# A two-layer hybrid trunk on one core: a gated delta net's planner costs, gating by halves, the order of Winograd splits and the places of operands

## The chip, the cores and the metric

The program runs on one core of one Trainium2 chip. The metric is the device time of one execution in microseconds. Five engines matter: PE (TensorE, the matrix products; PEld is its loading of the stationary operand), DVE (VectorE), ACT (ScalarE), POOL (GpSimd) and SP (SyncE, which issues most of the DMAs).

## The reference, cut to what matters

The input is a sequence of 1024 rows of 1024 numbers. Two layers are computed, each with a mixer and a feed-forward part, a modulation by a condition vector, and a layer norm after each part:

```python
e = jax.nn.silu(c @ cond_w + cond_b)
for i in range(DEPTH):                       # 2 layers
    mod = (e @ ada_w[i] + ada_b[i])[:, None, :]
    sh1, sc1, g1, sh2, sc2, g2 = jnp.split(mod, 6, axis=-1)
    y = mixers[i % N_MIXERS](x * (1.0 + sc1) + sh1)          # layer 0: gated delta net, layer 1: retention
    x = layer_norm(DN_ALPHA * x + (1.0 + g1) * y, ln_g[i, 0], ln_b[i, 0])
    y = conv_ffn(x * (1.0 + sc2) + sh2, ffn_up[i], ffn_conv_w[i], ffn_conv_b[i], ffn_down[i])
    x = layer_norm(DN_ALPHA * x + (1.0 + g2) * y, ln_g[i, 1], ln_b[i, 1])
```

The gated delta net has 8 heads of 128. Its projections q, k, v pass a short causal convolution and SiLU; q and k are normalised; per chunk a unit lower triangular system is solved, and a scan over the chunks carries a 128 x 128 state:

```python
kk = jnp.where(strict, jnp.einsum('bhncd,bhnmd->bhncm', kb, k) * decay, 0.0)
sol = lax.linalg.triangular_solve(kk + eye, rhs, left_side=True, lower=True, unit_diagonal=True)
v_new = u_n - jnp.einsum('bhck,bhkv->bhcv', w_n, state)
o = q_n * exp(g_n) @ state + qk_n @ v_new
state = state * jnp.exp(g_last)[..., None] + (k_n * exp(g_last - g_n))^T @ v_new
o = o * lax.rsqrt(jnp.mean(o * o, axis=-1, keepdims=True) + 1e-6) * norm_w
o = o * silu(z)                              # the gate; then o @ w_out
```

Retention has 4 heads with rotated q and k, 8 chunks of 128 and a normalisation of its output before a gate. The feed-forward part is `(silu(causal_dwconv(gate) + conv_b) * up) @ w_down` with 2816 hidden units.

## The kernel before, in words

Activations are kept transposed, features on the 128 partitions and time along the row, in two halves of 512. A product of full precision is made of three products of the faster type: each operand is split into a rounded high part (an ACT copy, line 89) and the rest (a DVE subtraction, line 90), by `split` (L88), and `mm3` (L108) or its like adds low times high, high times low and high times high. So each operand tile costs one ACT and one DVE pass before PE can use it. Instructions are emitted in program order, and a scheduler sets the order on each engine, from that order and from a model of when each is ready; only PE's order within `run` is fixed by the kernel itself.

*Delta net (about 80 to 620 us).* `run` (L725) is a planner: streams (Python generators) yield how long to wait on the planner's clock `clk`, or an event, and the ready stream of the lowest number goes next. Each product adds its cost to the clock (`pm`, `ptr`) and is chained behind the last on PE. The waits are in the table `LAT` (L1205). `filler` (L1150) has the last rank and emits the projections, one item of 48 products at a time (c: a tile of q, k or v; s: the same stored to memory for later; z: the gate's). For each quad of heads `t_path` (L843) makes the products `kk` and solves the 32 x 32 diagonal blocks on DVE (31 steps, transposes, three results RX, TX and T); `t_chain` (L913) copies these blocks to `T0` and `R` (by ACT, DVE and POOL) and joins them to 128 x 128 with products of 32 and 64 columns (`t1`, `t2`, `t3`); `prep` (L1006) transposes v and then k (`U`, whose `aux` places are given back after the scan); `dt_half` (L1027) makes the masked products `DT`; `scan` (L1050) goes over 8 chunks per head, four heads side by side, with the waits `s1`, `s2`, `s3`; `tail` (L1104) normalises four chunks, transposes them into `DT`'s tile and stores it to `oTd`. The second quad's `t_path` begins when the first quad's scans are done.

*Gating (L1224).* For each head the stored gate `zd` (512 KB) and both halves of `oTd` are loaded by SP, and DVE multiplies them in place. Then `proj_ln` (L312) makes the output projection, half of the rows at a time, with the weights' loads, four x rows' loads and background work (`bg_step`) as hooks; `bg_ada(0, 5, "row")` puts eight 512 KB loads of a modulation matrix and their DVE sums into that background (L1652).

*Feed-forward, up (L1266, `strassen`).* Weights of 256 columns and the activations are taken as 2 x 2 blocks in Winograd's form (`wino`, L1333): seven products of 12 matmuls each; the sums s1 to s4 of weight blocks are made by DVE in two PSUM banks in turn and each is split before its product. The results go to `sink`s: for the first item the gate with its convolution (`conv_q`, L1694: ACT copy L1699, two DVE sums L1704, ACT SiLU L1705), then the product with up (L1727). The same function makes the retention's q, k and gates, where the sink is the rotation (`rope_item`, 12 DVE operations an item, L1807 to L1812).

*Down projections and retention's output (L1408, `proj_gen`).* Seven products in Winograd's form again; each step `ops` (L1456) splits one activation block `ab` and one weight block `bb` into the tags "wl", "wr", "wh" (two places each) and, where `early`, "hTb". The last two steps of each product are kept as a tail and done by output tile. `early` holds in the first layer's down projection for the first five products, in the second's for all, in the retention's output projection for none.

*Retention (about 1735 to 2110 us).* The same planner runs `ret_v` as filler and `core` and `ret_back` per chunk, with the waits `RL` (L1981).

The lines at the planner's products and at the operands' places are these:

```python
def pm(out, lhsT, rhs, start=True, stop=True, cost=0.216):
    pq(pe.matmul(out, lhsT, rhs, start=start, stop=stop), cost)
...
at = ltags[0] if last and j >= nj - ltags[3] else ("wl", "hTb", "wr")[n % 3] if early else ("wl", "wr")[n % 2]
wt = ltags[1] if last and j >= nj - ltags[2] else ("wh", "hTb", "hTb")[n % 3] if early else "wh"
```

## Time and profile before

| what | value |
|---|---|
| median of 3 runs | 2921.36 us (2917.78 to 2926.29) |
| the profiled execution | 2919.49 us, its span 2917.7 us |
| mean granted clock of PE | 0.987 |
| busy: PE, DVE, ACT, POOL | 2799.6, 2183.0, 1299.3, 494.8 us |
| moved by DMA | 467.40 MB, 160 GB/s on the mean |

The span is from the first to the last instruction. "Busy" of an engine is the union of its instructions' times; matmuls are pipelined, so a busy PE is not at its peak. A wait's row names who waited, for what, the total in us, how often, and the longest. A window's row gives its length and then busy time and count for PE, PEld, DVE, ACT and POOL, then the granted clock of PE, the share of DMA and GB/s. A row of a timeline gives the start, the time it took, engine, line, operation, the tile written and those read, and in brackets the engine's idle time before it and what ended it. Rows of the chain in order of time give start, length and what was worked on.

### The profile page before, as it was taken

The numbers are of one execution on the slowest core, as the hardware profiler recorded it, in microseconds if no ns is written. First come the engines' busy times: TensorE is split into PE (matmuls) and PEld (weight loads), VectorE is DVE, ScalarE is ACT, GpSimd is POOL, SyncE is SP. The second block draws the span as 40 slices with busy tenths as digits, with TensorE's granted clock in tenths as the row PEclk, the third lists the DMA queues.
The fourth block names the chain that finished last, engine by engine and source line by source line (L and its number), as shares of the span: only waits on it lengthen the run. The fifth ranks groups of instructions, "written<-read, shape, count | busy, mean of one in ns | idle before, by whom it ended". The sixth has DMA issues, their size and how long they took to land.

```text
span 2917.7 us, 38768 instructions
## 1 busy us (share of the span) xinstructions
PE 2799.6 (96%) x13594; PEld 2288.3 (78%) x13594; DVE 2183.0 (75%) x3874; ACT 1299.3 (45%) x2387; POOL 494.8 (17%) x509
## 2 busy tenths in 40 slices
PE   8999999999999999998999999999999999999997
PEld 6787887877788788887877877777777788888886
DVE  6796678576789888768677665666688877777779
ACT  4754564444654444545333332222344644444543
POOL 0301311000023232200000022422202023331001
PEclk9998999999999999999999999999999999999999
DMA  7223332274355555855343374755664163434853
GB/s 282 94 79 100 123 127 81 80 255 150 104 170 170 191 182 168 292 163 169 130 148 115 117 241 150 215 169 173 196 220 144 55 201 134 143 128 162 289 181 116
DMA packets 252884, 467.40 MB, mean 160 GB/s; under 512 B 24144, under 2 KB 77776, under 8 KB 252688
## 3 DMA queue, kind: packets, MB, share of 16 engines
q1 hardware_dynamic: 217984, 409.07, 42.5%
q10 hardware_dynamic: 32064, 47.20, 4.4%
q0 software_dynamic: 2640, 8.65, 0.8%
q8 instruction: 107, 1.75, 0.3%
q14 instruction: 89, 0.73, 0.1%
HBM read 347.91 MB, written 116.92 MB: 159 GB/s over the span
## 4 chain that ended last, share of the span: by engine, by line
PE 68%; DVE 16%; DMA 8%; ACT 4%; issue 3%; POOL 1%; SPq 0%; ACTq 0%; DVEq 0%; POOLq 0%
PE acc L714 14%; PE acc L1272 8%; PE acc L110 5%; PE acc L111 5%; PE acc L112 5%; PE sc L1272 4%; PE acc L1570 4%; PE sc L714 4%; PE mm L714 3%; PE sc L110 2%; DVE o L1704 2%; PE sc L111 2%; PE sc L112 2%; DMA mvw<-in_ada_w 2%; DVE wb L90 2%
## 5 line engine op out<-in xcount | busy, mean ns | idle before, releaser
L714 PE MATMUL acc<-hT,wh 128*128 128x512 f32 x960 | 301.8, 396 | 0.0
L1570 PE MATMUL acc<-bb,ab 128*128 128x512 f32 x984 | 237.0, 399 | 14.1 <-DVE bb L90 12.4
L1570 PEld LDWEIGHTS acc<-bb,ab 128*128 128x128 f32 x984 | 186.8, 192 | 58.4 <-DVE bb L90 16.7
L714 PEld LDWEIGHTS acc<-hT,wh 128*128 128x128 f32 x960 | 184.1, 192 | 35.2
L1272 PE MATMUL acc<-T,wb 128*128 128x512 f32 x840 | 203.6, 391 | 8.3 <-DVE wb L90 8.1
L89 ACT ACTIVATE ab<-ar 128x512 fp32r<-128x512 f32 x210 | 130.2, 626 | 174.0 <-PE mm L303 46.5
L714 PE MATMUL acc<-hT,wl 128*128 128x512 f32 x480 | 200.6, 418 | 3.1 <-DVE wl L90 2.0
L90 DVE TENSOR_TENSOR ab<-ar,ab 128x512 fp32r<-128x512 f32 x210 | 147.6, 708 | 64.9 <-ACT ab L89 64.8
L411 POOL TENSOR_TENSOR xg<-xg,gb 128x512 f32<-128x512 f32 x48 | 63.6, 1327 | 772.2 <-DMA xg<-xs 468.7
L1272 PEld LDWEIGHTS acc<-T,wb 128*128 128x128 f32 x840 | 156.6, 188 | 46.2 <-DVE wb L90 11.1
L90 DVE TENSOR_TENSOR wl<-wr,wh 128x1024 fp32r<-128x1024 f32 x98 | 123.4, 1259 | 81.7 <-ACT wh L89 81.3
L89 ACT ACTIVATE wh<-wr 128x1024 fp32r<-128x1024 f32 x98 | 103.7, 1059 | 158.8 <-PE acc L714 60.0
L1735 POOL TENSOR_TENSOR o<-o 128x512 f32<-128x512 f32 x80 | 125.5, 1578 | 285.2 <-PE acc L112 185.2
L90 DVE TENSOR_TENSOR wb<-wr,wb 128x512 fp32r<-128x512 f32 x162 | 115.6, 718 | 71.9 <-ACT wb L89 71.7
L90 DVE TENSOR_TENSOR wb<-mm,wb 128x512 fp32r<-128x512 f32 x216 | 145.8, 684 | 25.3 <-ACT wb L89 24.5
L1704 DVE SCALAR_TENSOR_TENSOR o<-g,vc,o 128x512 f32<-128x512 f32 (+2 forms) x176 | 156.9, 909 | 4.4 <-ACT o L1699 3.8
L89 ACT ACTIVATE wb<-mm 128x512 fp32r<-128x512 f32 x216 | 124.3, 596 | 75.3 <-DVE mm L1326 71.3
L1342 ACT ACTIVATE pc<-acc 128x512 f32<-128x512 f32 x143 | 84.7, 592 | 139.4 <-PE acc L1272 91.4
L89 ACT ACTIVATE wb<-wr 128x512 fp32r<-128x512 f32 x162 | 98.6, 627 | 106.7 <-DMA wr<-in_ffn_up 45.8
L714 PE MATMUL acc<-wh,hT 128*128 128x512 f32 x384 | 135.0, 415 | 1.0 <-DVE vv L90 1.0
L110 PE MATMUL acc<-T,wb 128*128 128x512 f32 x292 | 115.3, 395 | 5.4 <-DVE wb L90 5.4
L239 DVE SCALAR_TENSOR_TENSOR ada<-mvw,e,ada 128x512 f32<-128x512 f32 x140 | 105.4, 753 | 18.2 <-DMA mvw<-in_ada_w 17.9
(671 smaller groups left out, 7375.5 us busy)
## 6 DMA issues: line engine op xcount, KB each, us to landing
wr<-in_ffn_up SPq DMA_DIRECT2D x92, 512.0 KB, 4.2
mvw<-in_ada_w SPq DMA_DIRECT2D x80, 512.0 KB, 4.5
ad<-o SPq DMA_DIRECT2D x154, 256.0 KB, 3.1
ar<-ad SPq DMA_DIRECT2D x154, 256.0 KB, 3.7
Br<-in_ffn_down SPq DMA_DIRECT2D x88, 256.0 KB, 3.4
wr<-in_ret_wv SPq DMA_DIRECT2D x32, 512.0 KB, 4.2
ar<-od SPq DMA_DIRECT2D x56, 256.0 KB, 5.3
wr<-in_gdn_wqkv SPq DMA_DIRECT2D x24, 512.0 KB, 3.5
```

Source lines behind the costliest of these rows:

```text
L89: act.activation(dst_h, src, AF.Copy)
L90: eng.tensor_tensor(dst_l, src, dst_h, ALU.subtract)
L110: mm(acc, wl[:, k], hl[0], start=first, stop=False)
L111: mm(acc, wh[:, k], hl[1], start=False, stop=False)
L112: mm(acc, wh[:, k], hl[0], start=False, stop=last)
L239: dve.scalar_tensor_tensor(a, wr[:, kk], e[:, k:k + 1], a, ALU.mult, ALU.add)
L714: pq(pe.matmul(out, lhsT, rhs, start=start, stop=stop), cost)
L1272: return pe.matmul(*a, skip_group_check=True, **kw)
L1342: act.activation(t, X, AF.Copy)
L1570: return pe.matmul(*args, skip_group_check=True, **kw)
L1704: dve.scalar_tensor_tensor(tv, gv[:, c0 - j:c1 - j], w[:, 2 - j:3 - j], tv, ALU.mult, ALU.add)
L1735: (dve if fp == 0 else pool).tensor_tensor(o[d], o[x], o[y], op)
```

## The change

Six things, in the order of the program:

- In the delta net the planner's costs of a product come from a table by its columns (`COST`), so 512 columns cost 0.229 instead of 0.216 and products of 32 and 64 columns 0.067 and 0.119 instead of 0.028 and 0.056. The retention's planner uses the same `pm`. The waits in `LAT` are changed, `kk` is shorter for the second quad, `prep` waits for the events `T0` of both pairs and then `v`, tails are staggered by head, `aux` is given back one chunk earlier.
- The filler's items stand in another order, and `fetch` loads and splits the weights of the next item before an item's products.
- The gating goes by halves: first all heads' first half, then the second; for heads 4 to 7 the second half is not stored and loaded but read from the tail's tile `DT`. `bg_ada(0, 5, "row")` is registered after the x loads of the first half's projection.
- In `wino` the second sum's split stands ahead of the third sum.
- The operands of `proj_gen` take the six places of "wl", "wr" and "wh" in turn where it is not early.
- In the first convolution of each up projection, the ACT copy is issued behind the newest split's ACT copy.

```diff
     def split(dst_h, dst_l, src, eng=dve):
-        act.activation(dst_h, src, AF.Copy)
+        anchor["sp"] = act.activation(dst_h, src, AF.Copy)
...
-            hooks = hooks + loads
+            hooks = hooks + loads + list(then)
...
-    def pm(out, lhsT, rhs, start=True, stop=True, cost=0.216):
-        pq(pe.matmul(out, lhsT, rhs, start=start, stop=stop), cost)
+    COST = {32: 0.067, 64: 0.119, 128: 0.224, HALF: 0.229}
+
+    def pm(out, lhsT, rhs, start=True, stop=True, cost=None):
+        pq(pe.matmul(out, lhsT, rhs, start=start, stop=stop), cost or COST[out.shape[-1]])
...
-                yield LAT["kk"]
+                yield LAT["kk"] - 0.4 * g
...
     def prep(p):
         heads = pairs[p]
-        yield after_ev(("T", p // 2), *[("f", 2 * GH + h) for h in heads])
+        yield after_ev(("T0", p & 2), ("T0", p | 1), *[("f", 2 * GH + h) for h in heads])
+        yield LAT["v"]
...
                 pm(p5, U[h][:, n], w)
+                if n == NCH - 2:
+                    give("aux", 1)
...
-        yield LAT["tail"]
+        yield LAT["tail"] + h % 4 * 0.8
...
-        act.dma_start(oTd[0][h, :, hs(q4)], flat(d))
+        if not (q4 and p > 1):
+            act.dma_start(oTd[0][h, :, hs(q4)], flat(d))
...
     def filler(items):
-        for kind, ti in items:
+        wnext = []
+
+        def fetch(i):
+            parked = set()
+            for j, (kind, ti) in enumerate(items):
+                if kind == "s":
+                    parked.add(ti)
+                elif kind == "h" or (kind == "c" and ti in parked):
+                    continue
+                if j >= i:
+                    wnext.append(load_w(A["gdn_wz" if kind == "z" else "gdn_wqkv"][ti]))
+                    return
+
+        for i, (kind, ti) in enumerate(items):
...
-            w = load_w(A["gdn_wz" if kind == "z" else "gdn_wqkv"][ti])
+            if not wnext:
+                fetch(i)
+            w = wnext.pop()
+            fetch(i + 1)
...
-    LAT = {"kk": 3.6, "exp": 3.2, "ld": 6.0, "g1": 12.0, "gm": 3.0, "mm": 2.2, "T": 6.0, "X": 3.4, "fs": 4.85, "T0": 8.0, "t1": 2.0, "t2": 3.3, "t3": 1.7, "D": 2.7, "s1": 1.9, "s2": 1.4, "s3": 1.8, "tail": 12.5, "ssq": 9.3, "fv": 4.0}
+    LAT = {"kk": 4.4, "v": 6.0, "exp": 3.2, "ld": 6.0, "g1": 12.0, "gm": 3.2, "mm": 2.2, "T": 6.0, "X": 11.0, "fs": 5.3, "T0": 10, "t1": 3.4, "t2": 3.3, "t3": 3.0, "D": 2.7, "s1": 1.4, "s2": 1.3, "s3": 1.6, "tail": 14.0, "ssq": 9.3, "fv": 4.0}
...
-    items = [("h", 1), ("h", 2), ("h", 3), (c, K + 2), (c, K + 3), (z, 0), (c, V), (c, V + 1), (c, V + 2), (c, V + 3), (c, 1),
-             (s, 2), (s, 3), (s, K + 4), (s, K + 5), (z, 1), (z, 2), (z, 3), (c, K + 4), (c, K + 5), (c, K + 6),
-             (c, K + 7), (s, 6), (s, 7), (c, V + 4), (c, V + 5), (c, V + 6), (c, V + 7), (c, 4), (c, 5),
-             (z, 4), (z, 5), (z, 6), (z, 7)]
+    items = [("h", 1), ("h", 2), ("h", 3), (c, K + 2), (c, K + 3), (z, 0), (s, 2), (c, 1), (s, 3), (c, V + 0), (c, V + 1), (c, V + 2), (c, V + 3), (s, K + 4), (s, K + 5), (z, 1), (z, 2), (c, K + 4), (c, K + 5), (c, K + 6), (c, K + 7), (z, 3), (s, 6), (s, 7), (c, V + 4), (c, V + 5), (c, V + 6), (c, V + 7), (z, 4), (c, 4), (c, 5), (z, 5), (z, 6), (z, 7)]
...
+    def gate_gdn():
+        raws = [two("qkv", F32, "raw") for _ in range(GH)]
+        for hf in range(2):
+            for k in range(0, GH, 2):
+                g = tl("aux", [P, 2, HALF], name="zg")
+                for j in range(2):
+                    sp.dma_start(g[:, j], zd[k + j, :, hs(hf)])
+                for j in range(2):
+                    raw = raws[k + j][hf]
+                    if hf and k + j in quads[1]:
+                        src = DT[k + j, 1]
+                    else:
+                        src = raw
+                        ld = sp.dma_start(raw, oTd[0][k + j][:, hs(hf)])
+                        if not hf:
+                            anchor["x", 0] = ld
+                    dve.tensor_tensor(raw, src, g[:, j], ALU.mult)
         return raws
...
             z5 = copy_of(Z)
+            w2 = block(s2)
             s4 = psub(a12, s2)
             drain(2)
-            prod(s2, "T2", X)
+            prod(None, "T2", X, w2)
...
-            at = ltags[0] if last and j >= nj - ltags[3] else ("wl", "hTb", "wr")[n % 3] if early else ("wl", "wr")[n % 2]
-            wt = ltags[1] if last and j >= nj - ltags[2] else ("wh", "hTb", "hTb")[n % 3] if early else "wh"
+            ring = ("wl", "wr", "wh")
+            at = ltags[0] if last and j >= nj - ltags[3] else ("wl", "hTb", "wr")[n % 3] if early else ring[2 * n % 3]
+            wt = ltags[1] if last and j >= nj - ltags[2] else ("wh", "hTb", "hTb")[n % 3] if early else ring[(2 * n + 1) % 3]
...
-            bg_ada(0, 5, "row")
...
-            xts = proj_ln(0, GH, get, wout, xsrc, G1, ("x", i))
+            xts = proj_ln(0, GH, get, wout, xsrc, G1, ("x", i), then=[lambda: bg_ada(0, 5, "row")])
...
-                act.activation(t, gv[:, hs(hf)], AF.Copy, scale=w[:, 2:3])
+                with after("sp") if fp == 0 else nullcontext():
+                    act.activation(t, gv[:, hs(hf)], AF.Copy, scale=w[:, 2:3])
```

## The prediction

> **What bounds the kernel now.** I read the page first, then the chain that ended last, then the waits of PE, then the stages by windows of time, and the timeline at each larger wait.

> ```profile
> span 2917.7 us, 38768 instructions
> PE 2799.6 (96%) x13594; PEld 2288.3 (78%) x13594; DVE 2183.0 (75%) x3874; ACT 1299.3 (45%) x2387; POOL 494.8 (17%) x509
> PEclk9998999999999999999999999999999999999999
> PE 68%; DVE 16%; DMA 8%; ACT 4%; issue 3%; POOL 1%; SPq 0%; ACTq 0%; DVEq 0%; POOLq 0%
> 813.77 2.72 PE acc L1272 x12
> ```

> PE is the bound: 96% busy, and most of the chain. Twelve 512-wide products in 2.72 us are 0.227 us each; where PE is never late that pace holds for whole stretches. The diff neither removes nor adds a product, so it can only win or lose time in which PE waits, or runs at the half clock that follows some waits. The third view names what PE waits for (total, times, longest).

> ```profile
> PE acc L1570 <- DVE bb L90: 12.4, 10, 4.8
> PE acc L1272 <- DVE wb L90: 8.1, 9, 1.1
> PE acc L717 <- DVE qkv L1014: 5.5, 1, 5.5
> PE acc L110 <- DVE wb L90: 5.4, 2, 2.7
> PE mm L717 <- DVE on L1938: 4.6, 4, 2.6
> PE acc L717 <- ACT sq L509: 4.4, 1, 4.4
> PE mm L714 <- DVE U L872: 2.9, 2, 1.5
> PE acc L714 <- DVE wl L90: 2.0, 2, 1.6
> ```

> The fourth view puts them in stretches: length, then busy time of PE, PEld, DVE, ACT and POOL, then the granted clock. I count as lost a stretch's length less PE's busy time, plus (1 - PEclk) times the length.

> ```profile
> 124.00:140.00 16.00, 11.74 (x59) 9.09 (x58) 13.68 (x54) 10.06 (x13) 3.28 (x4) 1.00 0.27 96
> 170.00:180.00 10.00, 8.42 (x37) 6.63 (x36) 8.32 (x15) 6.22 (x9) 0.18 (x2) 1.00 0.46 145
> 229.00:260.00 31.00, 25.48 (x392) 22.73 (x391) 23.10 (x45) 17.28 (x40) 8.50 (x22) 0.79 0.33 105
> 485.00:500.00 15.00, 10.04 (x105) 8.71 (x106) 11.56 (x20) 7.71 (x25) 4.46 (x9) 0.77 0.33 106
> 596.00:620.00 24.00, 24.00 (x132) 20.19 (x132) 16.27 (x39) 13.70 (x27) 3.02 (x3) 1.00 0.59 200
> 630.00:660.00 30.00, 25.80 (x110) 20.05 (x109) 24.53 (x35) 7.39 (x9) 0.00 (x0) 1.00 0.82 299
> 783.00:798.00 15.00, 11.20 (x42) 8.52 (x41) 13.93 (x24) 8.37 (x14) 0.00 (x0) 0.89 0.32 104
> 1320.00:1350.00 30.00, 25.21 (x106) 20.36 (x105) 24.94 (x53) 10.98 (x18) 4.13 (x4) 0.94 0.53 167
> 1364.00:1390.00 26.00, 22.83 (x100) 18.27 (x99) 22.99 (x39) 15.82 (x28) 0.59 (x1) 0.93 0.27 92
> 1480.00:1735.00 255.00, 248.13 (x1085) 202.60 (x1084) 180.03 (x285) 93.48 (x164) 16.12 (x12) 1.00 0.44 149
> 2036.00:2050.00 14.00, 11.25 (x51) 8.61 (x50) 11.02 (x21) 6.98 (x13) 0.82 (x2) 1.00 0.55 170
> 2110.00:2135.00 25.00, 20.99 (x89) 16.33 (x89) 23.89 (x39) 9.16 (x17) 0.00 (x0) 1.00 1.03 382
> 2185.00:2206.00 21.00, 18.49 (x77) 13.72 (x76) 21.00 (x42) 10.61 (x19) 0.50 (x1) 1.00 0.37 112
> 2305.00:2320.00 15.00, 11.32 (x41) 8.76 (x42) 15.00 (x25) 7.96 (x14) 0.00 (x0) 0.89 0.35 116
> ```

> In order (596 lost nothing) these lose 4.3, 1.6, 12.0, 8.4, 4.2, 5.5, 6.6, 5.0, 6.9, 2.8, 4.0, 2.5 and 5.3 us: 69 us that the change can reach. They are the ground of every term below.

> **The change part by part.**

> *`prep` waits for the `T0` blocks plus 6 us instead of `T`.* Before, its transposes of v (L717) follow directly on T, while ACT, DVE and POOL copy the diagonal blocks:

> ```profile
> 480.67 3.65 DVE L928 COPY R<-RX 32x128 f32<-32x128 f32 x8
> 485.10 2.83 DVE L928 COPY T<-TX 32x256 f32<-32x256 f32 x6
> 489.95 1.11 PE L717 MATMUL acc<-cst,qkv 128*128 128x128 f32 x4 [5.55 <-DVE qkv L1014]
> ```

> L1014, which must empty the accumulators, stands in DVE's queue behind both copy groups. The stretches at 229 and 485 lose 20.4 us; the idle part is 10.5, the rest half clock. Later transposes find DVE free, and filler products cover the copies. What is late next: the filler's own accumulators, which ACT frees. The scan is not delayed: v needs 6 + 4 x 2.2 planner us, less than `T0` plus `t1`, `t2`, `t3`. Ends 0 and -20.4; I take -12, since the small products at 247 stay.

> *`kk` 3.6 to 4.4 (4.0 in the second quad), `gm` 3.0 to 3.2.* More filler before the products that wait for L872 and L828; ends 0 and -4.3, taken -2.

> *`fetch` loads the next item's weights one item early.* Same loads and splits, moved ahead of one item of 48 products; the wait on wl is 2.0 us. A split that now stands ahead of a step of the chain in DVE's queue delays it by its own length. Ends +2 and -2, taken -1.5.

> *Gating by halves, last halves straight from `DT`, and the row of `ada` after the x loads.* 24 SP issues become 28 (zg halves, four raw loads fewer), 16 stores on ACT's queue become 12. SP's own issuing is 0% of the chain, so four more issues cost nothing while the filler lasts; without it each delays the load behind it. From 596 to 620 PE is busy 24.00 of 24.00, so gating earlier wins nothing there. The loss is behind it, 4.2 us at 630, where weights of the output projection wait behind loads of ada on SP:

> ```profile
> 631.63 8.70 DMA mvw<-in_ada_w
> ```

> Moving eight such loads back frees the weights; they meet later weights instead. Ends +4 and -4.2, taken -3.

> *The convolution's ACT copies behind the newest split (`after("sp")`).* At both starts of the Winograd part the convolution is ahead of the first sum's split:

> ```profile
> 783.93 1.40 DVE L1704 SCALAR_TENSOR_TENSOR o<-g,vc,o 128x512 f32<-128x512 f32 x2
> 785.26 0.68 DVE L90 TENSOR_TENSOR wb<-mm,wb 128x512 fp32r<-128x512 f32 x1
> 785.99 0.68 PE L110 MATMUL acc<-T,wb 128*128 128x512 f32 x1 [2.71 <-DVE wb L90]
> ```

> The stretches at 783 and 2305 lose 10.8 us together. Without L1704 ahead the split comes 1.4 us or more earlier, and the half clock after the wait goes too. Queued behind the new wait on ACT: L1699, and then the gate product L1727, which is needed later. Ends 0 and -10.8, taken -8. [...]

> *Six operand places in turn.* Only "not early" steps use it: the last two products of the first layer's down projection, and the whole retention output projection. Before, `bb` has two places ("wh"), both held by the tail of a product, so the next split on ACT waits for PE:

> ```profile
> 1339.39 0.63 ACT L89 ACTIVATE bb<-Br 128x512 fp32r<-128x512 f32 x1 [8.23 <-PE acc L1570]
> ```

> After, both operands have three; `ab` goes from four to three. In the first the stretches at 1320 and 1364 lose 11.6 us: ends +3 and -11.6, taken -8. In the second those at 2036, 2110 and 2185 lose 9.3: the first is partly DVE's queue of the retention, so -5 of ends +3 and -9.3.

> *Second sum's split ahead of the third sum.*

> ```profile
> ACT wb L89 <- DVE mm L1326: 71.3, 68, 2.6
> 1605.51 3.02 PE L1272 MATMUL sc<-T,wb 128*128 128x512 f32 x12 [1.06 <-DVE wb L90]
> ```

> ACT's split waits 68 times for a sum, and in the retention's projections (1480 to 1735) the second sum's product is late after rope items: 6.9 us. With the split first, DVE's part can go before the rope's operations. Ends +7 and -6.9, taken -5. [...]

> *Staggered tails (14 + 0.8 per head instead of 12.5), `aux` given back one chunk earlier, the filler's new order.* Nothing: filler products hide them (24.00 of 24.00 at 596). Without that cover the last tail, 16.4 planner us, would lie open behind the last scan; its price is in the slower rival.

> *Planner's costs.* These shift the order of PE in two stages.

> ```profile
> L714 PE MATMUL acc<-hT,wh 128*128 128x512 f32 x960 | 301.8, 396 | 0.0
> 609.54 0.39 PE L714 MATMUL mm<-w,DT 128*128 128x128 f32 x2
> 618.23 0.40 PE L714 MATMUL acc<-hT,wl 128*128 128x512 f32 x1
> ```

> A filler product costs 0.227 us; the planner takes 0.229 instead of 0.216. In the retention its waits `b`, `c` and `p` (6.51 us a chunk) are unchanged, so each chunk has 5.7% or 0.37 us less cover, at most 12 us over 32 chunks. There PE already waits for `on` 4.6 us in 4 places. Ends -1 and +12; taken +4.

> In the delta net a quad's waits on the chain add up, old: `kk` 28.8, `X` 3.4, `fs` 48.5, `T` 6, `T0` 8, `t1` to `t3` 7, `mm` 2.2, scan 37.1 = 141 planner us, or 148 real (x 0.227/0.216). New: 35.2 + 11 + 53 + 6 + 10 + 9.7 + 2.2 + 31.4 = 158.5, or 157 real; the second quad 154. So the chain grows by 15 us. The last scan ends at 609.5 and filler lasts to 618.5: 9 us of room, 6 short. Rounding each of 94 waits to a whole filler step of 0.69 us moves this both ways. Ends -9 and +60, taken +5, because after the filler the scan runs at its own pace.

> Sum: -12 -2 -1.5 -3 -8 -8 -5 -5 +4 +5 = -35.5 us. The profiled execution took 2919.5 us (span 2917.7 and 1.8 around it), 1.9 below the median of 2921.4. So 2884 on its scale, and 2886 on the median's.

> **The rivals.**

> *Waits move instead of going.* In the stretches of the sums, the ring and the convolution DVE is busy 13.93 of 15, 15.00 of 15 and 21.00 of 21 us: there it is the bound, and another order of its queue only makes another operand late (the third sum after the second). Then the 26 us of these four terms keep a quarter: -35.5 + 19.5 = -16, 2905 us. Against it: in the 255 us of 1480 DVE is busy only 180, and at 1339 it was ACT that waited, for a buffer.

> *All of it goes.* The 69 us less 9: -60, 2861 us. Against it: half clock after small products, and DVE full at three places.

> *The change does not do what it says:* the new order on DVE and ACT loses elsewhere what the waits gave, and it stays at 2921 within 8.

> *Slower: the filler runs out.* Place: the last scans, 560 to 620. If 94 waits are each rounded up by two thirds of a step, the chain grows by 43 more; 15 + 43 - 9 = 49 us idle, with clock lost as at 485 (0.23) 60 us in place of +5: -40.5 + 60 = +20, 2941 us. It decides from an overrun of 40 us on. For it: 1440 filler products (960 with wh, half as many with wl) are all there is. Against: scan waits shrink, and the first half of the projection can now follow before the second halves are done.

> **How the numbers follow.** A measurement here tells about 0.3% (9 us) from no change. Chances: forecast 0.50, waits move 0.22, all goes 0.08, no change 0.08, filler runs out 0.12. Faster 0.80, same 0.08, slower 0.12. The range reaches from all of it to no change, 2862 to 2922, and leaves out the slower case and half of the fastest. The likeliest case's own range is 2871 to 2901.

> **What would show it.** PE's waits on L1014 and on `sq` before L717 gone, the clock near 1.00 there; the waits on wb at L110 below 1 us; PE's waits on `bb` at L1570 under 5 us from 12.4; those on wb at L1272 under 4. Wrong would be: PE idle between the last scan product and the first L326, new waits on wb under L1272 with "22" operands, many waits on `on` or `Sr` in the retention.

## The result, and the profile after

The changed kernel takes 2905.0 us (median of 7) where the kernel before takes 2921.7: a ratio of 0.9946, 95% interval 0.9932 to 0.9960. A second set of runs gave 0.9963 (0.9952 to 0.9974). It is faster by 0.4 to 0.5%, 11 to 16 us, where 35.5 were forecast. The direction and the range held; the size did not. The profiled execution after took 2897.4 us, 7.6 below its median, so that a comparison of the two profiles alone flatters the change.

The first two lines of the page after:

```profile
span 2895.6 us, 38913 instructions
PE 2794.7 (97%) x13594; PEld 2284.7 (79%) x13594; DVE 2184.7 (75%) x3874; ACT 1295.0 (45%) x2387; POOL 490.4 (17%) x509
```

PE is still the bound. What it waits for after (total, times, longest):

```profile
PE acc L719 <- ACT oq L488: 5.5, 1, 5.5
PE acc L110 <- DVE wb L90: 4.2, 5, 1.6
PE acc L1285 <- ACT pc L1355: 4.0, 5, 1.7
PE acc L1585 <- DVE bb L90: 2.5, 1, 2.5
PE acc L716 <- ACT sq L509: 2.4, 1, 2.4
PE acc L1285 <- DVE wb L90: 2.2, 4, 1.1
PE mm L282 <- DMA xlo<-xs: 2.0, 1, 2.0
```

The announced rows went: bb 12.4 to 2.5, wb in the Winograd products 8.1 to 2.2, the 5.5 us on L1014 (now L1017) to 1.1. The row of wb at L110 only spread, 5.4 us in two waits to 4.2 in five with a longest of 1.6. In their place stand rows that the kernel before did not have or hardly had: 5.5 us at the transposes of the first quad on ACT's L488, 2.0 us on the loads of xlo, 4.0 us on ACT's pc. The same stretches as before, shifted to where their products stand now (length, busy PE, PEld, DVE, ACT, POOL, granted clock):

```profile
124.00:140.00 16.00, 13.76 (x69) 10.90 (x68) 14.52 (x50) 6.86 (x10) 4.19 (x5) 1.00 0.36 115
155.00:170.00 15.00, 12.16 (x60) 10.12 (x60) 12.80 (x41) 11.05 (x36) 2.32 (x3) 0.89 0.17 55
173.00:183.00 10.00, 10.00 (x50) 8.38 (x49) 7.59 (x18) 7.26 (x25) 3.12 (x5) 1.00 0.39 120
232.00:263.00 31.00, 25.52 (x223) 21.82 (x222) 26.11 (x47) 18.74 (x30) 9.94 (x21) 0.89 0.49 160
481.00:492.00 11.00, 11.00 (x52) 9.13 (x51) 8.89 (x17) 10.05 (x17) 9.82 (x22) 1.00 0.17 53
492.00:527.00 35.00, 31.46 (x457) 27.35 (x457) 19.48 (x42) 11.84 (x39) 0.18 (x1) 0.80 0.19 62
629.00:656.00 27.00, 26.53 (x116) 21.25 (x115) 23.28 (x33) 7.25 (x9) 0.00 (x0) 1.00 0.60 202
777.00:789.00 12.00, 10.75 (x47) 8.17 (x46) 11.39 (x20) 9.25 (x17) 0.00 (x0) 1.00 0.19 55
1466.00:1716.00 250.00, 246.90 (x1085) 202.97 (x1083) 178.99 (x286) 91.55 (x161) 17.13 (x12) 1.00 0.45 150
1716.00:1835.00 119.00, 112.79 (x500) 88.24 (x500) 66.02 (x108) 32.70 (x51) 35.90 (x37) 0.97 0.61 191
```

The convolution's start lost 5.5 us and now 1.25; the head of the output projection 4.2 and now 0.5; the retention's projections 6.9 and now 3.1. The stretch right behind those projections loses 6.2 + 0.03 x 119 = 9.8 us; before it lost 4.1 + 0.01 x 115 = 5.2 (row below). The stretch at 485 is clean where it lost 8.4, and the one behind it, at 492, now loses 3.5 + 0.20 x 35 = 10.5, before (500 to 535) 1.3 + 0.10 x 35 = 4.8. Over the whole delta net the granted clock did not gain: its stretches at one half add up to 34.1 us between 80 and 620 before, and to 34.1 in both profiles of the changed kernel.

```profile
1735.00:1850.00 115.00, 110.93 (x500) 86.76 (x499) 63.51 (x108) 31.88 (x50) 34.84 (x36) 0.99 0.59 184
```

Seventeen more kernels were run, and the changed one again. Each left a profile, so what a part does in a stage can be read over several executions. For the table I took, product by product in PE's order, the time from one end to the next less a pace for its shape (0.227 us for 512 columns, 0.111 for an instruction of 128, 0.06 for 64, 0.026 for 32; from one end to the next the profile of before has medians of 0.227, 0.111 and 0.058 and, for 32, a mean of 0.025), and added it over a stage, between the same products in every kernel. "Without" and "with" are means over the kernels that lack or have that part; the number of kernels is in brackets.

| stage (times of before) | forecast | without | with | found |
|---|---|---|---|---|
| delta net, 79-620 | -10.5 | 48.3 (7) | 51.6 (5) | +3.3 |
| output projection, 620-712 | -3 | 12.4 (5) | 7.2 (4) | -5.2 |
| two starts of the convolution | -8 | 12.4 (7) | 3.8 (7) | -8.6 |
| rest of the two feed-forward parts | 0 | 14.9 (6) | 14.9 (5) | 0 |
| down projection, 1320-1390 | -8 | 11.2 (7) | 7.8 (7) | -3.4 |
| retention's projections, 1480-1735 | -5 | 10.3 (8) | 3.2 (6) | -7.1 |
| retention's run | +4 | 15.9 (7) | 24.2 (2) | +8.3 |
| retention's output | -5 | 13.4 (7) | 9.2 (7) | -4.2 |
| norm and start behind it, 2206-2306 | 0 | 11.5 (7) | 12.3 (7) | +0.8 |
| sum | -35.5 | | | -16 |

The sum agrees with the time of the first set. Single profiles of one group differ (by 6 to 7 us in the delta net, by 5 in the down projection), so a row of 3 us is not far above chance. The missing 19 us are in three rows, the delta net (14), the down projection (5) and the retention's run (4), less 4 that the others won beyond their terms.

### The profile page after: what moved, and what is told of

Same layout as the page of the kernel before. It is cut to its first block, busy times and chain, and to the rows that moved or that the text cites. A ratio compares the mean times of both kernels' runs of the same rounds, so it can differ in the third digit from the quotient of the medians.

```text
span 2895.6 us, 38913 instructions
## 1 busy us (share of the span) xinstructions
PE 2794.7 (97%) x13594; PEld 2284.7 (79%) x13594; DVE 2184.7 (75%) x3874; ACT 1295.0 (45%) x2387; POOL 490.4 (17%) x509
## 4 chain that ended last, share of the span: by engine, by line
PE 54%; DVE 23%; DMA 10%; issue 6%; ACT 5%; POOL 1%; SPq 0%; ACTq 0%; DVEq 0%; POOLq 0%
PE acc L716 9%; PE acc L1285 5%; PE acc L1585 4%; PE acc L110 4%; PE acc L111 4%; PE acc L112 4%; PE sc L716 3%; PE sc L1285 3%; DVE o L1719 3%; PE mm L716 2%; DMA mvw<-in_ada_w 2%; DVE wb L90 2%; DMA wr<-in_ffn_up 2%; DVE qkv L490 2%; DVE mm L1339 2%
## 5 line engine op out<-in xcount | busy, mean ns | idle before, releaser
L1585 PE MATMUL acc<-bb,ab 128*128 128x512 f32 x984 | 230.9, 393 | 6.9 <-DVE ab L90 3.3
L89 ACT ACTIVATE ab<-ar 128x512 fp32r<-128x512 f32 x210 | 131.1, 629 | 220.9 <-PE mm L303 48.3
L90 DVE TENSOR_TENSOR ab<-ar,ab 128x512 fp32r<-128x512 f32 x210 | 149.0, 715 | 81.4 <-ACT ab L89 81.3
L1285 PE MATMUL acc<-T,wb 128*128 128x512 f32 x840 | 202.1, 389 | 0.4 <-DVE wb L90 0.4
L89 ACT ACTIVATE wb<-mm 128x512 fp32r<-128x512 f32 x216 | 124.1, 597 | 167.3 <-DVE mm L1339 158.8
L90 DVE TENSOR_TENSOR wl<-wr,wh 128x1024 fp32r<-128x1024 f32 x98 | 123.3, 1258 | 82.8 <-ACT wh L89 82.5
L89 ACT ACTIVATE wh<-wr 128x1024 fp32r<-128x1024 f32 x98 | 103.6, 1060 | 148.3 <-PE acc L716 60.1
L90 DVE TENSOR_TENSOR wb<-wr,wb 128x512 fp32r<-128x512 f32 x162 | 114.1, 705 | 64.1 <-ACT wb L89 64.0
L1750 POOL TENSOR_TENSOR o<-o 128x512 f32<-128x512 f32 x80 | 112.5, 1414 | 269.0 <-ACT pc L1355 175.2
L90 DVE TENSOR_TENSOR wb<-mm,wb 128x512 fp32r<-128x512 f32 x216 | 145.2, 686 | 6.9 <-ACT wb L89 6.9
L1339 DVE TENSOR_TENSOR mm<-wr 128x512 f32<-128x512 f32 x108 | 87.8, 813 | 76.7 <-DMA wr<-in_ffn_up 61.3
L89 ACT ACTIVATE wb<-wr 128x512 fp32r<-128x512 f32 x162 | 101.3, 626 | 94.0 <-PE acc L1285 28.4
```

Of the source, the lines that this page charges most:

```text
L89: anchor["sp"] = act.activation(dst_h, src, AF.Copy)
L90: eng.tensor_tensor(dst_l, src, dst_h, ALU.subtract)
L1285: return pe.matmul(*a, skip_group_check=True, **kw)
L1339: dve.tensor_tensor(t, x, y, op)
L1585: return pe.matmul(*args, skip_group_check=True, **kw)
L1750: (dve if fp == 0 else pool).tensor_tensor(o[d], o[x], o[y], op)
```

## The experiments

Ratios are to the kernel before, run on the same chip, with 95% intervals; 0.001 is 2.9 us.

**Three late parts together, and each alone.** Edit: the kernel before with the convolution's copies behind the newest split (first two pairs of lines), the second sum's split in front of the third sum, and the six operand places; then with each of the three alone.

```diff
-        act.activation(dst_h, src, AF.Copy)
+        anchor["sp"] = act.activation(dst_h, src, AF.Copy)
...
-                act.activation(t, gv[:, hs(hf)], AF.Copy, scale=w[:, 2:3])
+                with after("sp") if fp == 0 else nullcontext():
+                    act.activation(t, gv[:, hs(hf)], AF.Copy, scale=w[:, 2:3])
...
+            w2 = block(s2)
             s4 = psub(a12, s2)
             drain(2)
-            prod(s2, "T2", X)
+            prod(None, "T2", X, w2)
...
+            ring = ("wl", "wr", "wh")
```

> The kernel before with three parts of the change alone: the convolution's ACT copies behind the newest split, the six operand places, and the second sum's split ahead of the third sum. My terms for these were -8, -13 and -5. Theory A (these waits really go; what failed lies elsewhere): about -24 us, a ratio of 0.991 to 0.993; the stretches that lost 5.5 and 5.3 us before the first products on a sum lose about 2 each, the wait of PE for bb in the down projection falls from 12.4 to under 4 us. Theory B (waits move instead of going, the rival on record): -7 us, a ratio near 0.998, with new waits on wb or on ACT's results of about the size of the old ones.

> The kernel before with the second sum's split ahead of the third sum alone. My term was -5. Theory A: -5 us, 0.998, the 9 us lost in the retention's projections fall to 3 and nothing answers. Theory B (the wait moves): 0 to +3 us, 1.000 to 1.001; the projections lose 5 to 6 us less, and PE then waits 2 to 4 us for xlo at its first transposes (L282), because SP still stands in front of the row stores whose products POOL makes, and loses 5 to 8 us more between there and the retention's fifth chunk.

> The kernel before with the convolution's ACT copies behind the newest split alone. My term was -8. If the wait is gone for good: -7 to -9 us, 0.997, with 1.8 us lost in each of the two starts instead of 6. If it moves on to the sums behind it: the starts lose 1.8 each all the same, the 80 us behind each start lose 3 to 4 us more than before, and the time is -1 to -3 us, 0.999 to 1.000.

> The kernel before with the six operand places in turn alone. My terms were -8 in the down projection and -5 in the retention's output. If both hold: -13 us, 0.9955. If the down projection's 11.6 us were the bad luck of one execution (kernels with the old places lose 8.5 to 14.0 there, 11.0 in the mean, those with the new ones 7.6): -3.4 -4.4, so -8 us, 0.997 to 0.9975, and less if the time won at the retention's output is waited for at the start of the next feed-forward part, where all kernels with the new places lose 3 to 9 us more.

Measured: together 0.9964 (0.9952 to 0.9976), -10.5 us. Alone: the second sum's split 0.9995 (0.9981 to 1.0009), the convolution's copies 1.0007 (0.9994 to 1.0019), the six places 0.9988 (0.9976 to 0.9999). The three alone add up to -3 us, together they give -10.5, nearer theory B than theory A. Each of the four figures is known to some 3.5 us, so that the difference is only just clear of noise by the times alone; that these parts need each other is borne out by the windows, and below by the changed kernel without the second sum's split. First come the copies alone, at the first start and in the stretch behind it; then that stretch in the kernel before; then the three together:

```profile
783.00:794.00 11.00, 9.62 (x41) 7.26 (x41) 10.97 (x18) 8.08 (x15) 0.00 (x0) 1.00 0.26 78
794.00:881.00 87.00, 84.44 (x366) 69.01 (x365) 71.94 (x109) 38.32 (x72) 21.47 (x17) 0.98 0.50 172
```

```profile
798.00:880.00 82.00, 82.00 (x365) 67.92 (x364) 68.39 (x104) 38.92 (x72) 21.39 (x16) 1.00 0.51 174
```

```profile
789.00:872.00 83.00, 82.94 (x366) 68.03 (x366) 69.88 (x110) 39.53 (x74) 21.44 (x16) 1.00 0.54 183
```

Alone, the start wins its 4 us (1.4 lost, from 5.5) and the next 87 us give them back: 2.6 idle plus 0.02 x 87 of clock, where before nothing was lost. PE's longest wait in that stretch names the next late operand:

```profile
PE sc L1272 <- DVE wb L90: 1.9, 1, 1.9
```

The convolution was late either way; put behind the first split, it now delays the second sum's. With that split in front of the third sum as well, the stretch is clean (82.94 of 83). So the -8 was right at its two places in every kernel that has the part, and worth nothing without the term that I priced beside it as if the two were independent.

The second sum's split alone gains its 7 us in the projections and pays them back at the first transposes of the retention, where PE waits for the loads of xlo. The timeline of that kernel around it:

```profile
1714.64 4.73 SPq L413 DMA_DIRECT2D xg<-xg  x2
1717.73 1.29 POOL L412 TENSOR_TENSOR xg<-xg,gb 128x512 f32<-128x512 f32 x1
1722.08 0.94 SPq L1840 DMA_DIRECT2D xlo<-xs  x2
1729.01 0.69 PE L282 MATMUL mm<-cst,xlo 128*128 128x128 f32 x2 [5.15 <-DMA xlo<-xs]
```

SP stands in front of the store of a row (L413) until POOL has multiplied it, at 1719.0; only then come the loads. Rows and POOL did not get faster with PE, so PE reaches the transposes 5 us early and waits 5.15.

**The row stores off SP.** Edit: in the changed kernel, gained rows are stored from POOL's queue.

```diff
-            (sp if tag == "lane" else pool).dma_start(dst[rs, hs(c)], x)
+            pool.dma_start(dst[rs, hs(c)], x)
```

> The changed kernel, unaltered, beside the three edits of it that follow, on the same chip: 0.993 to 0.996 of the kernel before. All theories say the same; it shows how far one execution of it differs from another by stage.

> The changed kernel with one edit: the gained rows that POOL multiplies during the retention's projections (L413) are stored from POOL's own DMA queue and no longer from SP's. If PE's wait for xlo (2.0 to 5.1 us in every kernel with the second sum's split in front) comes from SP standing in front of these stores: that wait falls under 0.5 us, the half clock behind it (3.4 us of it or 6.8) goes, and the time falls by 3 to 6 us against the changed kernel, to 0.992 to 0.9935 of the kernel before. If the loads of xlo are late because the 16 DMA engines are full there: the wait stays at 2 us or more and the time within 2 us. A loss is possible where POOL pays for each store itself: up to +5.

Measured: the changed kernel again 0.9963 (0.9952 to 0.9974), the edit 0.9977 (0.9965 to 0.9990). PE's wait for xlo is gone (it was 2.0 and 4.4 us in the two profiles of the changed kernel); the time does not fall. The loads now start 8.5 us ahead of the first transposes, where they had 3.8 and 2.1 us up to the time PE was ready. But in this profile the projections also lose 6.5 us instead of 3.1 to 4.0, so PE comes some 3 us later, which alone would hide most of that wait. What the 6.5 comes from was not followed up. That SP stands in front of the stores is shown by the timeline; how much of PE's wait it makes, this run does not separate.

**The changed kernel without the second sum's split.**

```diff
-            w2 = block(s2)
...
-            prod(None, "T2", X, w2)
+            prod(s2, "T2", X)
```

> The changed kernel without the second sum's split in front of the third sum. If the gain in the projections is repaid at xlo and in the first feed-forward (+2.4 -6.9 +7.7 by stage): 1 to 4 us faster than the changed kernel, 0.993 to 0.996, no wait of PE for xlo over 0.5 us. If my -5 was right in this kernel: 4 to 6 us slower, 0.997 to 0.998.

Measured: 0.9999 (0.9983 to 1.0014), some 10 to 15 us slower than the changed kernel. My expectation that it would be faster is refuted. In its place: the projections lose 10.3 again, and the stretches behind the two starts lose nearly what they lost with the copies alone (84.12 busy of 86 us at 0.98):

```profile
795.00:881.00 86.00, 84.12 (x365) 68.92 (x364) 70.05 (x109) 38.69 (x72) 20.19 (x16) 0.98 0.52 175
```

**The planner's cost in the retention.** Edit: in the changed kernel the retention plans with 0.216 us again.

```diff
+    for c in (128, HALF):
+        COST[c] = 0.216
     run([(0.0, ret_fill())] + [(-1.0, core(h)) for h in range(RH)])
```

> The changed kernel with the old planner cost of 0.216 us for 128 and 512 columns in the retention alone. My term for the new cost was +4, bound +12. By stage the two traces show +8 between the first and the last product of the retention's run. If that comes from the new cost: 5 to 8 us faster than the changed kernel, so a ratio to the kernel before of 0.992 to 0.993 where the changed kernel has 0.9946, and PE's wait for on at L1953 falls from 6.9 us in 5 places to about 4.6 in 4. If it was the chance of one execution: no difference, 0.9946.

Measured: 0.9965 (0.9949 to 0.9982), no difference. The retention's run loses 24.1 us with the old cost and 22.5 and 25.9 with the new one. The second sum's split alone makes 23.6 of 15.9 (4 kernels, old cost); the new cost alone, in the kernel without that split, 21.4 (one kernel). So either makes the run 5 to 8 us worse, and both together no worse than one.

**The delta net's part, alone and left out.** Edit: the kernel before with everything of the delta net's plan; the kernel before with prep's wait alone; the changed kernel without all of the delta net's plan; the changed kernel with prep's old wait.

```diff
-        yield after_ev(("T", p // 2), *[("f", 2 * GH + h) for h in heads])
+        yield after_ev(("T0", p & 2), ("T0", p | 1), *[("f", 2 * GH + h) for h in heads])
+        yield LAT["v"]
```

> The kernel before with the delta net's whole part of the change alone: prep's wait, the six costs and all the planner's waits, the filler's order and its weights one item early, aux one chunk earlier, staggered tails. The retention keeps the old costs. My terms for this added up to -10.5 us (-12 -2 -1.5 +5). Theory A (the two traces by stage): between 0 and -3 us, a ratio of 0.999 to 1.000, because the wait in front of the first quad's small products stays at 5 us under another name and half clock moves into the second quad's small products. Rival (the difference of the two profiles is the chance of one execution): -8 to -11 us, 0.996 to 0.997.

> The kernel before with one edit: prep waits for the T0 blocks plus 6 us and no longer for T. My term was -12. If the edit itself gains and the rest of the new planning loses it again: -7 to -12 us, a ratio of 0.996 to 0.9975. If the gap only moves, because the filler's own accumulators then wait for an ACT that is busy with the T copies: -4 us to 0, with a PE wait of some 5 us on a result of L488 or L491 in place of the one on L1014, in one quad at least.

> The changed kernel without the delta net's part: the delta net's order, waits and costs are those of before; gating by halves, the ada row behind the x loads, the convolution's copies, the six places and the second sum's split are in. Theory A (the delta net's part is a loss of 6 to 11 us, which the changed kernel carries): -20 to -28 us against the kernel before, 0.9905 to 0.993, so faster than the changed kernel's 0.9946. Rival (the parts do not add: in the changed kernel the gating gains only because the delta net's new order ends in its favour): -9 to -16 us, 0.9945 to 0.997.

> The changed kernel with prep's old wait put back: its transposes of v follow on T again, and the 6 us go. My term for the new wait was -12; alone on the kernel before it measured +7. If it is a loss in itself: 4 to 8 us faster than the changed kernel. If the rest of the delta net's new planning needs it (the longer waits for T0, the fuller filler): 5 to 10 us slower, with the 5.9 us in front of the second quad's transposes back.

Measured: the whole plan alone 1.0029 (1.0016 to 1.0042), +8.5 us; prep's wait alone 1.0022 (1.0011 to 1.0033), +6.4; all but the plan 0.9947 (0.9927 to 0.9968), as fast as the changed kernel; the old wait in the changed kernel 0.9968 (0.9955 to 0.9981), no difference. In the kernel before, PE stood in the first quad already for accumulators that ACT frees, behind ACT's copies of the blocks to R:

```profile
231.97 3.42 ACT L930 ACTIVATE R<-RX 32x128 f32<-32x128 f32 x8 [0.33 <-DVE RX L898]
236.72 1.12 PE L717 MATMUL acc<-cst,qkv 128*128 128x128 f32 x4 [4.41 <-ACT sq L509]
```

Prep's wait with nothing else, in the first quad:

```profile
238.74 3.87 ACT L930 ACTIVATE T<-TX 32x256 f32<-32x256 f32 x6
242.63 0.28 ACT L509 ACTIVATE sq<-acc 128x128 f32<-128x128 f32 x1
243.17 2.18 PE L717 MATMUL acc<-cst,qkv 128*128 128x128 f32 x8 [3.80 <-ACT sq L509]
```

Now the filler's next transposes ask ACT for accumulators, and the copies to T0 stand in ACT's queue for 3.87 us. PE stops for 3.80 us, little less than before. In the second quad, where PE did ask DVE before, it now asks ACT, and L491 starts at 495.72, as ACT's six copies end. So what I named as late next and priced at nothing stands in both quads. The waits of the second, and the copies ahead of them:

```profile
PE acc L717 <- ACT qkv L491: 3.3, 1, 3.3
PE acc L717 <- ACT sq L509: 1.1, 1, 1.1
491.74 3.95 ACT L930 ACTIVATE T<-TX 32x256 f32<-32x256 f32 x6 [0.24 <-DVE TX L902]
```

And the half clock got longer:

```profile
232.00:263.00 31.00, 27.20 (x388) 24.43 (x387) 20.07 (x42) 16.11 (x40) 8.61 (x22) 0.66 0.32 104
501.00:534.00 33.00, 32.96 (x496) 30.14 (x494) 17.09 (x42) 8.41 (x20) 0.00 (x0) 0.74 0.15 50
```

In the second of these PE is busy 32.96 of 33 us and has the clock at 0.74. The wait now stands right in front of the 32x32 products, and the clock stays at one half through them: 23.9 us in one piece in the first quad and 20.5 in the second, 47.8 in the delta net where the kernel before had 34.1. PE waits less than before, and the time is longer.

**Taking the copies away from the filler's accumulators.** Edit: prep's wait alone, with the first pair's T0 copies on POOL; and the changed kernel with its copies issued in steps, filler between them.

```diff
-                block(T0[bs, hh, :, cs], TX[bs, :, ch].rearrange("p i c -> p c i"))
+                src = TX[bs, :, ch].rearrange("p i c -> p c i")
+                if p % 2:
+                    dve.tensor_copy(T0[bs, hh, :, cs], src)
+                else:
+                    pool.tensor_copy(T0[bs, hh, :, cs], src)
```

In steps, with T0's own wait 4 instead of 10:

```diff
                 block(T0[bs, hh, :, cs], TX[bs, :, ch].rearrange("p i c -> p c i"))
+            yield 2.0
...
                         pool.tensor_copy(Rv[bs, :, bs], src)
+            if not hh:
+                yield 2.0
```

> The kernel with prep's wait alone (measured +7 us), with one more edit: the first pair's T0 blocks are copied by POOL and no longer by ACT, so ACT's queue is about 3.9 us shorter between the small products' start and the squares that free the filler's accumulators. Theory C (prep's gap moved to the accumulators that ACT frees): PE's wait for sq at L717 (3.8 us) falls under 1.5, the half clock in front of the small products falls from 24 and 20 us to 10 or less, and the time falls by 5 to 9 us against prep's wait alone, to 0.999 to 1.000 of the kernel before. Rival D (the small products themselves keep the clock low, or POOL is now late with the T0 blocks): no gain, 1.002 or above, with PE waiting for T0 or R before the small products.

> The changed kernel with the diagonal blocks' copies issued in steps: 2.0 planner us of filler after each head's T0 copies and between the two heads' R copies, and T0's own wait 4 instead of 10. Theory C (the gap in front of the small products is the copies standing in ACT's and DVE's queues in front of what frees the filler's accumulators): PE's wait at L719 for L488 (5.5 us) falls under 2.5, the half clock around the first quad's small products falls from 17 us to 10 or less, and the time falls by 3 to 7 us. Rival D (the small products themselves keep the clock at half, whatever stands in front of them): the wait falls, the half clock stays at 14 us or more in both quads, and the time within 3 us.

Measured: with POOL 1.0023 (1.0010 to 1.0037), no better. The wait leaves the first quad, where PE now waits for POOL's copies, and in the second it is longer (a row of each):

```profile
PE mm L714 <- POOL T L943: 3.0, 3, 2.3
PE acc L717 <- ACT sq L509: 5.8, 1, 5.8
```

Rival D's second half, POOL late with the blocks, is what happened in the first quad; with the copies on POOL, PE stands for POOL there. The copies in steps: 0.9987 (0.9974 to 1.0000), 7 us slower than the changed kernel. There the gap is gone, and the clock falls all the same (1.00, then 0.50):

```profile
245.00:255.00 10.00, 10.00 (x124) 8.48 (x123) 9.21 (x15) 6.95 (x11) 6.13 (x15) 1.00 0.26 67
251.79:255.21 3.42, 3.42 (x104) 3.07 (x103) 2.57 (x5) 1.78 (x4) 0.00 (x0) 1.00 0.61 134
255.21:279.10 23.89, 20.91 (x294) 19.42 (x290) 12.20 (x29) 6.15 (x11) 0.11 (x1) 0.50 0.47 159
```

PE is busy 10.00 of 10 us, and then 23.89 us are at 0.50. Nothing stood still in front of them; 100 of the products in the last 3.42 us ahead of them are the 32x32 ones.

**Dense products among the small ones.** Edit: in the changed kernel the filler issues its next three 512-wide products behind every eight 32x32 products; then behind every eight 64x64 ones as well; then the first without the second sum's split. fill() lets the filler take one step, if it can.

```diff
                     pm(pa[h3, c0:c0 + 32], U[h][l3, n, h3], T0[l3, hh, n, 0:32])
+                fill()
...
+                    if n % 4 == 3:
+                        fill()
```

> The changed kernel with one edit: behind every eight 32x32 products of the delta net the filler issues its next three 512-wide products (0.69 us), so that no 3.4 us of PE hold small products alone. Same products, same waits. Theory E (32x32 products don't keep the clock up, even when PE never waits): the half clock between 250 and 280 and between 500 and 525 falls from 17.1 and 13.7 us to 3.4 or less each, and the time falls by 6 to 12 us against the changed kernel (0.9946 and 0.9963), to 0.991 to 0.993. Theory C (only the gaps in front make the half clock): half clock stays within 4 us of what it was, time within 3 us.

> The same, and one such step of the filler behind every eight 64x64 products too. Theory E: as with the small ones alone, half clock gone there, and up to 2 us more for the 64-wide stretch, or up to 3 us lost because the chain waits for the filler's steps and the scans end later.

> Both edits: dense products among the 32x32 ones, and the second sum's split where it was. If both theories hold, their gains add: 0.990 to 0.992, the fastest of all. If either fails it is no faster than the better of the two alone.

Measured: 1.0057 (1.0041 to 1.0073), 1.0037 (1.0020 to 1.0055) and 1.0088 (1.0071 to 1.0105): 22 to 37 us slower than the changed kernel's 0.9963. The three windows of the first, the small products of both quads and the end of the delta net:

```profile
258.00:279.00 21.00, 21.00 (x246) 15.15 (x245) 5.49 (x8) 4.79 (x8) 0.10 (x1) 0.93 0.45 152
500.00:530.00 30.00, 26.84 (x298) 18.91 (x297) 13.66 (x20) 13.42 (x41) 0.23 (x2) 1.00 0.23 72
601.00:646.00 45.00, 33.73 (x195) 28.68 (x194) 34.97 (x93) 22.60 (x54) 6.28 (x6) 0.74 0.73 249
```

and the same products in the changed kernel, in its second profile:

```profile
248.00:279.00 31.00, 24.40 (x412) 21.95 (x412) 20.90 (x45) 11.30 (x18) 3.93 (x9) 0.72 0.39 129
504.00:527.00 23.00, 22.26 (x407) 20.23 (x404) 10.16 (x28) 5.14 (x15) 0.00 (x0) 0.70 0.08 26
```

The clock goes from 0.72 and 0.70 to 0.93 and 1.00, with no other edit than dense products among the small ones: in these runs the half clock goes with small products that stand alone. The time is lost elsewhere: the last scan product starts only at 634.1 (changed kernel 607.1 and 609.3), the filler has run out at 612, and the last scans stand alone from 601 to 646 with 11.3 us idle and 0.26 x 45 = 11.7 us of clock. That is the slower rival of the prediction, brought about by another edit: 23 us, where it reckoned with 49 us idle and 60 in all.

**Gating by halves alone.**

```diff
-    raws = gate_phase(A["gdn_wz"], 0, GH, ["qkv"] * GH, zearly)
+    raws = gate_gdn()
```

> The kernel before with gating by halves, the last halves straight from DT, and the ada row behind the x loads. My term was -3, ends +4 and -4.2. Theory A: -3 to -7 us, 0.9975 to 0.999, with the waits before the first products of the output projection (2.0 and 2.1 us lost at 634 and 646) gone. Rival (without the delta net's new order the halves come too late and the gate works behind DVE's scan): 0 to +4 us.

Measured: 1.0009 (0.9996 to 1.0022). The head of the output projection is clean there, and the stretch ahead of it is not:

```profile
621.00:639.00 18.00, 13.97 (x57) 11.60 (x58) 11.73 (x17) 5.30 (x9) 3.16 (x1) 0.91 0.63 220
639.00:662.00 23.00, 23.00 (x101) 18.70 (x100) 19.81 (x29) 6.37 (x9) 0.00 (x0) 1.00 0.57 179
```

```profile
PE acc L717 <- DVE qkv L1112: 4.4, 1, 4.4
```

PE waits 4.4 us for the last tail's normalized rows. Their way over DVE and POOL in that kernel:

```profile
617.73 0.68 DVE L1109 TENSOR_REDUCE so<-DT 128x4 f32<-128x512 f32 x1
618.93 1.29 DVE L90 TENSOR_TENSOR hl<-raw,hl 128x512 fp32r<-128x512 f32 x2
620.13 0.16 DVE L1110 SCALAR_TENSOR_TENSOR so<-so,ssq 128x4 f32<-128x4 f32 x1
620.43 3.73 POOL L1111 TENSOR_TENSOR so<-so,mhalf 128x4 f32<-128x4 f32 x1 [13.79 <-DVE so L1110]
624.19 0.69 DVE L1112 TENSOR_TENSOR qkv<-qkv,so 128x512 f32<-128x512 f32 x1 [0.90 <-POOL so L1111]
```

The row sums stand 1.7 us behind a product of the gate and two of its splits on DVE, and POOL's power takes 3.73 us more. In the changed kernel that wait is not there:

```profile
607.07 0.39 PE L716 MATMUL mm<-w,DT 128*128 128x128 f32 x2
617.31 0.69 DVE L1116 TENSOR_TENSOR qkv<-qkv,so 128x512 f32<-128x512 f32 x1 [0.90 <-POOL so L1115]
```

Its last normalised rows start at 617.31, and at 618.34 in its second profile, against 624.19. The scans' end explains little of it: the last scan product starts at 607.07 and 609.32, with the gate alone at 609.71 and before at 609.54. Most is won in the tail itself, where the rows follow that product by 10.2 and 9.0 us instead of 14.5 (POOL's power takes 2.53 and 1.41 us there). Which of the plan's edits does that was not tried.

So the delta net's plan gains nothing in the delta net (+3.3), and makes room for the gate: with both, the output projection loses 7.2 us, with the gate alone 12.4, with the plan alone 14.3. The two nearly cancel, and the kernel without the plan is as fast.

## Why the prediction was wrong

- **Prep, -12: the step that failed.** "What is late next: the filler's own accumulators, which ACT frees" was written down and priced at nothing. That wait is 3.8 us in the first quad and 3.3 and 1.1 in the second, and 5.5 in the changed kernel; instead of -12 the edit alone measured +6.4. The first quad's stretch was misread as well: PE waited there for ACT already (4.41 us for sq), not for L1014, which was the second quad's wait alone. And the half clock did not go with the waits: with prep's wait alone it lay on the small products in pieces of 23.9 and 20.5 us, 47.8 us of half clock instead of 34.1.
- **kk, gm and fetch, -3.5:** their two stretches are better (2.2 and 0 us lost at 124 and 173), but at 155 PE waits 2.4 us for sq, and 2.8 us idle and 1.7 of clock are lost between 155 and 170. Nothing is left of them in the stage's sum.
- **The delta net's planner, +5:** the overrun that it was for did not come. The sum of waits said that the chain grows by 15 us; the last scan product starts 2.5 and 0.2 us earlier than before in the two profiles of the changed kernel. Which of the waits were overestimated was not tried.
- **Output projection, -3:** found -5.2, but only with the new plan in front of it. Something in that plan, whose tails were priced at nothing, is what the gate needs: the last tail's rows come 6 to 7 us earlier with it.
- **Convolution, -8:** -8.6 at its places, and given back behind them unless the second sum's split goes in front as well. The row of 0.89 in both starts is 1.00 after.
- **Six places, -8 and -5:** -3.4 and -4.2, and alone -3.5 in time. The mechanism was right (bb 12.4 us to 2.5); the first size was read off one execution. That stretch lost 14.0 in the profile of before and 8.5 to 13.0 in six other kernels with the old places.
- **Second sum's split, -5:** -7.1 in its stage. The reckoning ended with the stage: the retention's run then starts before its loads, and loses 7.7 more. The +4 for the planner's cost does not add to that.
- **"Waits move instead of going":** its 2905 us is the time measured, but by luck, not for its reason. It had the sums, the ring and the convolution keep a quarter; together they keep 10.5 of 26. The larger part was lost in the delta net, where the rival kept everything. Its mechanism is what the copies, the second sum's split, prep's wait and the gate showed when each stood alone.

## What to carry to other kernels

When an engine's wait is removed, the next operand in line can set the time at once, as it did here (1.9 us on the next wb behind the convolution's copies, 5.15 on xlo behind the second sum's split); name it, read its own lateness from the queue that it stands in, and subtract that before booking the gain. Parts that reorder the same queue (here copies, first, second and third sums on DVE and ACT) are to be priced together: three parts that measured 3 us one by one, each to some 3.5, measured 10.5 as one. No kernel tried was faster than the changed one; the one without the delta net's plan was as fast. A loss read off a single execution may be off by several microseconds (the down projection lost 8.5 to 14.0 with the same places); size it from several executions that share the stage's code.

## What the runs showed of the hardware

```profile
246.85:250.26 3.41, 3.41 (x113) 3.26 (x113) 2.67 (x4) 1.10 (x2) 0.00 (x0) 1.00 0.80 298
502.84:506.25 3.41, 3.41 (x172) 3.24 (x171) 2.10 (x5) 0.24 (x1) 0.00 (x0) 1.00 0.02 5
```

These two are of the kernel before (112 and 167); the other three, from 265.36, 504.29 and 511.12 in the changed kernel, hold 183, 114 and 166. With 52 and 82 of them (before, from 496.02 and 499.43) and with 84 and 69 (after, from 258.53 and 261.94), full clock followed. Half clock also follows two stretches of before in which PE does nothing at all:

```profile
233.19:236.60 3.41, 0.00 (x0) 0.00 (x0) 3.33 (x8) 3.33 (x15) 3.01 (x9) 1.00 0.20 74
485.78:489.19 3.41, 0.00 (x0) 0.00 (x0) 3.32 (x6) 2.96 (x5) 3.17 (x7) 1.00 0.00 0
```

So in these profiles it came behind idle time and without any. Full clock was back behind 3.41 us that held six 512-wide products (before at 263.91 and 277.56, after at 279.01), and once behind 3.41 us with 34 of the 32x32 and 12 of 128 columns (after at 511.12). With three 512-wide products among every eight small ones the mean was 0.93 and 1.00. The 32x32 products lost less by half clock than the larger: from one start to the next 31 ns at full clock and 47 at half (medians of the kernel before), against 111 and 213 for 128 columns and 227 and 427 for 512. What the clock so held is worth is not shown: all three kernels with dense products among the small ones are slower.
